# Handing sums of a two-level Strassen-Winograd matmul from PSUM bank to PSUM bank with ScalarE's copies, and two more products in quarters

## The chip, the cores and the metric

One core of one Trainium2 chip runs the whole kernel. The metric is the time of the device in microseconds; of the kernel before, three runs were timed, with a median of 1532.32 us (1531.6 to 1532.37). The core's engines are TensorE (PE, with its weight loads PEld), VectorE (DVE), ScalarE (ACT), GpSimd (POOL) and SyncE (SP). TensorE adds into PSUM, eight banks of 512 fp32 columns for each of 128 partitions.

## The reference

```python
m, k, n = 4096, 4096, 4096
a, b: float32, drawn from a normal distribution; alpha = 0.01
x = np.matmul(a, b)
return np.where(x > 0, x, alpha * x)
```

A product of two 4096 x 4096 matrices, and a leaky ReLU on the result, in fp32 in and out.

## The kernel before

The operands are rounded to fp16. The output is worked in sixteen regions of 1024 x 1024, named (g, j): g is the group of 1024 rows of A, j the group of 1024 columns of B. Region (0, 0) is an ordinary matmul, done while the inputs begin to arrive. The other fifteen follow one another in one loop, in the order (0,1), (0,2), (0,3), (1,2), (1,0), (1,3), (1,1), (2,2), (2,0), (2,3), (2,1), (3,2), (3,0), (3,1), (3,3). Each of them is a 2 x 2 block product over K = 2 x 2048, done in Winograd's form of Strassen's algorithm: seven products of [512 x 2048] by [2048 x 512] in place of eight. A row group's last region, where the next group's rows of A arrive, is called turning ((0,3), (1,1), (2,1)).

The seven products are in code `product(0)` to `product(6)`; here they are the first to the seventh. The list PRODUCTS names their operands: A11, A12, S2, S3, S1, A22, S4, where the S are sums of blocks of A, against blocks of B or sums T of them, which VectorE makes in place. A whole product is 64 matmuls of 128 x 512, over 16 chunks of K and 4 row tiles, each row tile adding in a PSUM bank. The first, third and fifth product add into the four banks y, which carry the running sum from one to the next. The second, fourth and sixth use the other four banks, z. The seventh adds onto y again. y and z change places from region to region.

What leaves a region:
- block C11 is the first product plus the second. ScalarE copies the first product out of y to SBUF (`keep`, giving u1), and VectorE adds the second product's banks to it. A leaky step follows and a store (`leave`).
- the third product's running sum is kept as u2, the fourth product as v. u2 + v and the fifth make the other blocks with the sixth and the seventh.

Many products are done once more by the same scheme, one level down, as seven "quarters": 7 x 16 matmuls of 128 x 256, 112 in all. These are the sixth and the seventh product of the ten regions that are neither of group 0 nor turning (`in_quarters`), the fourth of those among them that are not the first of their group (`in_fourth`) and of the turning ones of groups 1 and 2, and the fifth of the regions in the list FIFTH, which holds (2, 3) alone. The sums that the quarters need of a block of A are made once per row group, kept in DRAM (kept_q) and loaded again in each region; those of B are made by VectorE each time. The fourth, sixth and seventh quarters' results go from their bank to SBUF by ScalarE's copies and VectorE's adds (`more`, and the adds at line 1219).

The order of the work is written out by hand: within each engine and each queue instructions run in the order of the program text, and an engine that waits holds up all that is behind it. Semaphores between engines follow from the tiles: who writes or reads a bank waits for those before it that touch the same bank. These places matter below:
- Line 1101 and lines 1113 to 1116: regions in the list EARLY begin with one measurement of B (two in (2, 0) and (3, 1)). A measurement is four squares on ScalarE (line 231) and VectorE's additions of them (lines 240 to 243), with the fourth square and the next measurement waiting for VectorE to free a buffer. They stand in ScalarE's queue ahead of the first product's copies.
- `judge` (line 619) looks at what was measured. Its second half, some twelve small VectorE instructions, stands in the last region, (3, 3), ahead of the fifth product.
- `load_sums` (line 754) loads sums of A: on SP's queue for the sixth product, each into a buffer whose last reader must have ended; on ScalarE's queue, by `following`, for the seventh.
- `seventh_at_the_end` (line 992) is the last region's seventh product; its first quarter writes two banks at once, `one` and `one_more`, that is zbank + 3 and zbank + 1.
- `z6` at line 1271 gives the order in which the sixth product gets its banks; after a fifth in quarters it is (0, 2, 1, 3).

Of the kernel before, what the change touches and what calls it, by code (L numbers as in the profile page):

```python
# [31 lines left out]
MT = 4  # L32
# [16 lines left out]
def kernel(  # L49
# [17 lines left out]
    nc = tc.nc  # L67
# [274 lines left out]
    for what, i, *more in order:  # L342
        if what == "a":
            r, tiles = more
# [320 lines left out]
    FIFTH = {(2, 3)}  # L665
# [127 lines left out]
    for i, (g, j) in enumerate(regions):  # L793
# [14 lines left out]
        def product(n, banks, first):  # L808
# [26 lines left out]
        def fourth_in_quarters(banks, tq, sx):  # L835
# [11 lines left out]
            if not turning:  # L847
                quarter_product(sx[4], b[1, 1], into(other), True)
# [7 lines left out]
            if turning:  # L856
                quarter_product(sx[4], b[1, 1], into(other), True)
            return pairs, kept, [(block(r, n), pair(bank)) for r, n, bank in (
                (0, 0, fourth), (0, 1, other), (0, 1, third), (1, 0, one), (1, 1, one))]

# [43 lines left out]
        def sixth_in_quarters(pairs, banks, v_pairs, v, y, tq, sq, between=None):  # L904
# [4 lines left out]
            one, other, third, fourth = banks  # L909
# [13 lines left out]
            quarter_product(x[0, 0], b[0, 0], into(one), True)  # L923
            add(v[:2], y[:2])
            more(0, 0, one)
            add(v[2:], y[2:])
            quarter_product(sx(1), t(1), into(other), True)
            more(1, 1, other)
# [9 lines left out]
            more(0, 1, one)  # L938
            if between:

                leave(v_pairs, 1, 1, (0,))
                t3_of_b(y7)
            sums_of_b(y7, next_t, (2,))
            more(0, 0, fourth)
            quarter_product(sx(4), b[1, 1], into(other))
            following(1, sq.get("room"))
            next_t[4] = tq[2]
            more_t4 = lambda: sums_of_b(y7, next_t, (4,))
            if not between:
                more_t4()  # L950
            more(0, 1, other)
            quarter_product(sx(3), b[0, 1], into(one))
            following(3, sq.get("last"))
            more(1, 0, one)
            more(1, 1, one)
            quarter_product(x[1, 1], t(4), into(third), True)
            if between:
                more_t4()
            more(1, 0, third)
# [162 lines left out]
        u1_pairs, u1 = keep(y, side)  # L1122
# [23 lines left out]
        product(1, z, True)  # L1146
# [5 lines left out]
        add(u1, z)  # L1152
# [3 lines left out]
        if in_fourth:  # L1156
            tq = {n: new_a16() for n in (2, 4)}
# [7 lines left out]
            sums_of_b(quarters_of_b(i, 0, 1), tq, (4,))  # L1165
# [21 lines left out]
        if in_fourth:  # L1187
            tq[1] = t[:, 3]
            sums_of_b(quarters_of_b(i, 0, 1), tq, (1,))
# [21 lines left out]
        if in_fourth or turning and g:  # L1211
            v_pairs, v, parts = fourth_in_quarters(z, tq, {**s3_rooms(g), 4: a_quarter(sx4)})
            if turning:
                for n in range(3):
                    turn_a_in(0, 1, n)
            for n, (to, bank) in enumerate(parts):
                if in_fifth and n == 2:
                    sums_of_b(quarters_of_b(i, 0, 0), t5, (1,))
                nc.vector.tensor_add(to, bank, to)
                if in_fifth and n == 0:  # L1220

                    t3_of_b(quarters_of_b(i, 0, 0))
                    sums_of_b(quarters_of_b(i, 0, 0), t5, (2, 4))
            if turning or in_fifth:
                add_v()
        else:
# [84 lines left out]
        if not in_quarters:  # L1311
            product(5, z, g > 0)
            add(u2[::-1], z[::-1])
# [115 lines left out]
```

## Time and profile before

| | |
|---|---|
| median of three runs | 1532.32 us (1531.6 to 1532.37) |
| span of the profiled execution | 1531.4 us, 21934 instructions |
| TensorE: matmuls | 8715 |
| VectorE busy | 1171.2 us (76%) |
| ScalarE busy | 428.1 us (28%) |
| granted TensorE clock over the span | 1.000 |
| HBM read, written | 347.61 MB, 117.44 MB |

The profiled execution is read by its span, from the first to the last instruction; 0.9 us lie between that span and the median of the runs. PE is the matmul, L819 a whole product's and L762 a quarter's; L832 is ScalarE's copy out of a bank, L1041 VectorE's add of a bank to kept sums, L917 the sixth product's adds, L231 a square, L754 a load of sums of A. A row of the timeline has the start and the length in us, the engine, the line, the operation with its tiles and shapes and how many were merged; in brackets stands how long the engine had been idle before and what ended that. The chain of waits has start, length and what was on it. In the table of groups stand the busy time, the mean of one in ns, then the idle time before them and what ended it.

### The profile page before, as it was taken

What the parts mean: (1) busy time and instruction counts of PE and PEld (TensorE: products, weight loads), DVE (VectorE), ACT (ScalarE), POOL (GpSimd) and SP (SyncE); (2) the same over time, 40 slices, a digit from 0 to 9 for tenths busy, and PEclk for the clock granted to TensorE, in tenths of its full rate; (3) what the DMA queues carried; (4) which work ended last, traced back from release to release, by engine and by line L of the source; (5) the groups of instructions that cost most, each with busy time, mean ns of one, the idle gap of its engine ahead of it and who ended that gap; (6) DMA issues with size and microseconds to landing.
All of it is one profiled execution on the core that took longest, in us unless ns stands there. A gap on an engine that the chain in (4) does not pass through costs nothing. (4 is left out here: it accounts for less than half of the span.)

```text
span 1531.4 us, 21934 instructions
## 1 busy us (share of the span) xinstructions
PE 1521.0 (99%) x8715; PEld 851.5 (56%) x8715; DVE 1171.2 (76%) x1231; ACT 428.1 (28%) x734; POOL 258.2 (17%) x426
## 2 busy tenths in 40 slices
PE   9999999999999999999999999999999999999998
PEld 4444444444446567574544747577544475746656
DVE  4378867766897676768789599688978868687677
ACT  2201334646310213103651130313464103041210
POOL 5641110143202011022220001000331100101000
PEclk9999999999999999999999999999999999999999
DMA  9999995998979999899898939859999892948824
GB/s 248 188 216 200 239 281 168 180 193 176 251 312 257 277 237 276 243 290 246 184 310 279 302 149 231 294 154 343 217 241 297 229 347 70 295 161 189 302 97 140
DMA packets 194258, 356.50 MB, mean 233 GB/s; under 512 B 18913, under 2 KB 132833, under 8 KB 181090
## 3 DMA queue, kind: packets, MB, share of 16 engines
q0 software_dynamic: 119808, 112.22, 46.4%
q1 hardware_dynamic: 67714, 217.22, 38.0%
q10 hardware_dynamic: 6624, 25.56, 4.4%
q8 instruction: 70, 1.15, 0.3%
q14 instruction: 42, 0.34, 0.1%
HBM read 347.61 MB, written 117.44 MB: 304 GB/s over the span
## 5 line engine op out<-in xcount | busy, mean ns | idle before, releaser
L819 PE MATMUL ps<-b,a 128*128 128x512 f16 x2624 | 570.7, 379 | 1.4 <-DMA b<-in_b_dram 1.4
L819 PE MATMUL ps<-b,s 128*128 128x512 f16 x2176 | 475.2, 379 | 0.0
L819 PEld LDWEIGHTS <-a 128*128 128x128 f16 x2624 | 256.7, 98 | 309.3 <-issue 1.7
L819 PEld LDWEIGHTS <-s 128*128 128x128 f16 x2176 | 212.8, 98 | 255.2 <-issue 0.4
L592 DVE TENSOR_TENSOR b<-b 128x4096 f16<-128x4096 f16 x104 | 234.8, 2286 | 46.0 <-DMA b<-in_b_dram 34.1
L536 POOL DMA_DIRECT2D b<-in_b_dram x128 | 94.8, 745 | 879.8 <-PE ps L762 448.2
L832 ACT COPY c<-ps 128x512 f32<-128x512 f32 x164 | 85.0, 596 | 483.2 <-PE ps L819 439.2
L142 DVE STREAM_TRANSPOSE a<-a 128x512 uint32<-128x512 uint32 (+2 forms) x120 | 127.0, 1105 | 78.9 <-DMA a<-in_a_dram 78.9
L133 POOL DMA_DIRECT2D a<-in_a_dram x252 | 137.4, 553 | 245.5 <-ACT junk L611 73.6
L762 PEld LDWEIGHTS <-q 128*128 128x128 f16 x1488 | 145.6, 98 | 16.9
L313 DVE SCALAR_TENSOR_TENSOR c<-c 128x1024 f32<-128x1024 f32 (+2 forms) x123 | 141.8, 1194 | 4.1 <-ACT c L832 3.8
L611 ACT ACTIVATE junk<-a 128x512 bf16<-128x512 f16 x192 | 121.1, 631 | 83.4 <-DMA a<-in_a_dram 78.1
L1041 DVE TENSOR_TENSOR c<-ps,c 128x512 f32<-128x512 f32 x140 | 87.5, 683 | 62.8 <-PE ps L819 51.2
L231 ACT ACTIVATE sq<-b 128x2048 bf16<-128x2048 f16 x64 | 118.4, 1910 | 38.8 <-DVE sq L240 31.0
L762 PEld LDWEIGHTS <-a 128*128 128x128 f16 x1200 | 117.4, 98 | 17.4
L283 PE MATMUL ps<-b,a 128*128 128x512 f16 x512 | 112.2, 379 | 0.5 <-ACT a L380 0.2
L762 PE MATMUL ps<-b,q 128*128 128x256 f16 x816 | 95.6, 273 | 0.0
L762 PE MATMUL ps<-b,a 128*128 128x256 f16 x752 | 88.3, 273 | 0.0
L283 PEld LDWEIGHTS <-a 128*128 128x128 f16 x512 | 49.7, 98 | 60.8 <-issue 1.4
L977 ACT COPY c<-ps 128x512 f32<-128x512 f32 x9 | 5.3, 586 | 255.6 <-PE ps L762 145.8
L762 PEld LDWEIGHTS <-s 128*128 128x128 f16 x672 | 65.7, 98 | 7.6
L762 PE MATMUL ps<-q,q 128*128 128x256 f16 x544 | 64.6, 273 | 0.0
(108 smaller groups left out, 917.0 us busy)
## 6 DMA issues: line engine op xcount, KB each, us to landing
b<-in_b_dram POOLq DMA_DIRECT2D x136, 512.0 KB, 11.8
out_dram<-c SPq DMA_DIRECT2D x240, 256.0 KB, 7.0
a<-in_a_dram POOLq DMA_DIRECT2D x244, 128.0 KB, 5.7
b<-kept_half SPq DMA_DIRECT2D x28, 1024.0 KB, 11.8
b<-kept SPq DMA_DIRECT2D x20, 1024.0 KB, 8.8
q<-kept_qs ACTq DMA_DIRECT2D x40, 512.0 KB, 7.8
s<-kept_s SPq DMA_DIRECT2D x18, 1024.0 KB, 7.6
q<-kept_qa SPq DMA_DIRECT2D x28, 512.0 KB, 7.5
```

The source lines that it names most:

```text
L133: nc.gpsimd.dma_start(a16[32 * q:32 * q + 32], src.rearrange("(g i) w -> i g w", i=32))
L142: nc.vector.transpose(part.rearrange("p c m e -> p c (m e)").bitcast(U32) .rearrange("p c (g i) -> p g c i", i=32), src[:, :, i * n:(i + 1 ...
L231: nc.scalar.activation(to, self.parts[n], SQUARE)
L283: nc.tensor.matmul(ps, a_cols(at[0, h, u], c, mt, (h, u) == (0, 0)), bt[0, u, nt][:, c, :], start=first, stop=last,)
L313: nc.vector.scalar_tensor_tensor(t, t, alpha, t, op0=MULT, op1=MAX if alpha <= 1 else MIN)
L536: nc.gpsimd.dma_start(t[:, c:c + 4, :], b_rows(j, u, c, 4, nt, g > 0))
L592: nc.vector.tensor_tensor(f(to), f(x0), f(x1), op)
L611: nc.scalar.activation(junk, piece[:, q, :], SQUARE, accum_out=to[:, 4 * n + q:4 * n + q + 1])
L762: nc.tensor.matmul(to[m], xq[:, c // 2, rows, c % 2], yq[:, c, :], start=first and c == 0 and m < banks, stop=c == KC - 1, skip_group_chec ...
L819: nc.tensor.matmul(banks[mt], a_cols(t, c, mt, t is first_a), B(half, nt, k)[:, c, :], start=first and (k, c) == todo[0], stop=(k, c) == t ...
L832: nc.scalar.copy(kept[mt], banks[mt])
L1041: nc.vector.tensor_add(to, bank, to)
```

## The change

- `FIFTH` becomes (2, 3), (3, 1), (3, 3): the fifth product of two more regions is done in quarters. With it go, as in group 2, the sums of S1 in region (3, 0), their stores and loads, and in (3, 3) the second half of `judge` comes after the fifth product.
- C11: ScalarE copies the first product's banks y into the banks z, and the second product adds onto them; the whole block is then kept by ScalarE's copies. VectorE's four adds go. The last sixteen matmuls of the first product and the first sixteen of the second are ordered by bank.
- The fourth product in quarters of the regions `in_fourth` becomes `fourth_by_seeds`: sums that several blocks share are copied by ScalarE from bank to bank, and the quarters that follow add onto the copy. VectorE's adds at the end go from five to two, and T's sums 1 and 4 change places in time. The turning regions keep `fourth_in_quarters`.
- The sixth product in quarters is reordered and seeded in the same way: two copies into bank `one`, one into `other`; VectorE's `more` go from eight to six; the order of the quarters, of the loads for the seventh and of VectorE's sums changes.
- In the turning regions of groups 1 and 2 ScalarE copies u2 (with v in it) into z, the sixth product adds onto it, and ScalarE copies it back.

```diff
-    FIFTH = {(2, 3)}
+    FIFTH = {(2, 3), (3, 1), (3, 3)}
...
             order = [(mt, k, c) for k, c in todo for mt in range(MT)]
+            if n == 0:
+                order[-16:] = [(mt, k, c) for mt in range(MT) for k, c in todo[-4:]]
+            elif n == 1:
+                order[:16] = [(mt, k, c) for mt in range(MT) for k, c in todo[:4]]
             if n == 0 and late_s2:
...
+        def fourth_by_seeds(banks, tq, sx):
...
+            chain, shared, one, other = banks
...
+            quarter_product(x[0, 0], b[0, 0], into(chain), True)
+            nc.scalar.copy(one, chain)
+            quarter_product(sx[1], t(1), into(shared), True)
+            quarter_product(sx[2], t(2), into(chain))
+            nc.scalar.copy(other, chain)
+            quarter_product(x[0, 1], b[1, 0], into(one))
+            nc.scalar.copy(block(0, 0), pair(one))
+            quarter_product(sx[3], b[0, 1], into(chain))
+            nc.scalar.copy(one, chain)
+            nc.scalar.copy(block(1, 1), pair(chain))
+            quarter_product(sx[4], b[1, 1], into(other))
+            nc.scalar.copy(block(0, 1), pair(other))
+            quarter_product(x[1, 1], t(4), into(one))
+            nc.scalar.copy(block(1, 0), pair(one))
+            return pairs, kept, [(block(r, 1), pair(shared)) for r in (1, 0)]
...
         def sixth_in_quarters(...)
-            one, other, third, fourth = banks
+            chain, shared, one, other = banks
...
+            quarter_product(x[0, 0], b[0, 0], into(chain), True)
+            nc.scalar.copy(one, chain)
+            add(v, y)
+            quarter_product(sx(1), t(1), into(shared), True)
             following(4)
             next_t[2] = tq[1]
-            quarter_product(x[0, 1], b[1, 0], into(fourth), True)
             if between:
                 next(between)
+                leave(v_pairs, 1, 1, (0,))
+                t3_of_b(y7)
             else:
                 leave(v_pairs, 1, 1)
-            quarter_product(sx(2), t(2), into(one))
+            quarter_product(sx(2), t(2), into(chain))
+            nc.scalar.copy(other, chain)
             following(2)
+            sums_of_b(y7, next_t, (2,))
+            quarter_product(x[0, 1], b[1, 0], into(one))
+            more(0, 0, one)
+            next_t[4] = tq[2]
+            if not between:
+                sums_of_b(y7, next_t, (4,))
+            for r in (0, 1):
+                more(r, 1, shared)
+            quarter_product(sx(3), b[0, 1], into(chain))
+            nc.scalar.copy(one, chain)
+            more(1, 1, chain)
+            following(1, sq.get("last"))
+            quarter_product(sx(4), b[1, 1], into(other))
             if between:
+                sums_of_b(y7, next_t, (4,))
             more(0, 1, other)
+            following(3, sq.get("room"))
+            quarter_product(x[1, 1], t(4), into(one))
             more(1, 0, one)
...
-        u1_pairs, u1 = keep(y, side)
+        for mt in range(MT):
+            nc.scalar.copy(z[mt], y[mt])
...
-        product(1, z, True)
+        product(1, z, False)
...
-        add(u1, z)
+        u1_pairs, _ = keep(z, side)
...
+            if in_fifth:
+                t3_of_b(quarters_of_b(i, 0, 0))
+                sums_of_b(quarters_of_b(i, 0, 0), t5, (2, 4, 1))
...
             if turning or in_fifth:
                 add_v()
+            if turning:
+                z = [new_bank(zbank + mt) for mt in range(MT)]
+                for mt in range(MT):
+                    nc.scalar.copy(z[mt], u2[mt])
...
-            product(5, z, g > 0)
-            add(u2[::-1], z[::-1])
+            product(5, z, False)
+            if g:
+                for mt in range(MT):
+                    nc.scalar.copy(u2[mt], z[mt])
+            else:
+                add(u2[::-1], z[::-1])
```

More of the change, by code (lines that the diff above doesn't have):

```diff
@@ L943, in sixth_in_quarters @@
[L943 to L950, printed above, removed]
+            sums_of_b(y7, next_t, (2,))
[4 more added lines that the diff above has]
+                sums_of_b(y7, next_t, (4,))
@@ L954, in sixth_in_quarters @@
+            quarter_product(x[1, 1], t(4), into(one))
             more(1, 0, one)
[L955 to L959, printed above, removed]
             next_t[1] = tq[4]
@@ L1211 @@
         if in_fourth or turning and g:
-            v_pairs, v, parts = fourth_in_quarters(z, tq, {**s3_rooms(g), 4: a_quarter(sx4)})
+            fourth = fourth_by_seeds if in_fourth else fourth_in_quarters
+            v_pairs, v, parts = fourth(z, tq, {**s3_rooms(g), 4: a_quarter(sx4)})
             if turning:
```

34 lines of the change are left out of this document (10 added, 24 removed).

## The prediction

> **What bounds the kernel now.** I read the busy times first, then the chain that ended last.
>
> ```profile
> PE 1521.0 (99%) x8715; PEld 851.5 (56%) x8715; DVE 1171.2 (76%) x1231; ACT 428.1 (28%) x734; POOL 258.2 (17%) x426
> ```
>
> ```profile
> 945.38 33.41 DMA b<-in_b_dram
> 978.79 0.04 issue
> ...
> 1303.03 13.81 PE ps L819 x64
> 1316.85 24.45 PE ps L762 x224
> 1341.30 41.44 PE ps L819 x192
> ```
>
> TensorE is the bound, and a busy share that counts pipelined matmuls would prove little; the chain does. After one wait for a load of B, ended at 978.79, it is TensorE alone up to the last additions: a whole product takes 13.81 us for 64 matmuls (0.2158 each), two in quarters 24.45 us, so 12.23 us each and 1.747 us per quarter. The reader is to see that nothing else is on the path, so VectorE's 1171 us and ScalarE's 428 us cost nothing today. Work taken from VectorE therefore gives nothing by itself. What counts is how many matmuls go, and whether a new wait stops TensorE.
>
> **The change part by part.**
>
> *Two more fifth products in quarters.* In regions (3, 1) and (3, 3), 64 matmuls of 512 columns become 112 of 256: 2 × (13.81 − 12.23) = **−3.2 us**. This is the only work taken from TensorE. What it adds elsewhere (four sums of S1 on VectorE and their stores in region (3, 0), four sums of B and some ten small adds in each of the two regions, about 8 MB of copies) lies beside TensorE, whose cover is the whole products 3 and 5 around it; costed at nothing. Without that cover it would cost its VectorE time, about ten microseconds a region.
>
> *C11 handed on, the ordinary seam.* ScalarE now copies the first product's four banks into the second product's, and the second product adds onto them. Before, TensorE went from one to the other with no such wait. The new order ends bank m of the first product 4 matmuls (0.86 us) before bank m + 1 and begins the second product in the same way; where the fourth sum is loaded late the first two banks end 3.45 us early as they do now. Four copies fit:
>
> ```profile
> L832 ACT COPY c<-ps 128x512 f32<-128x512 f32 x164 | 85.0, 596 | 483.2 <-PE ps L819 439.2 <-DMA out_dram<-c 27.7 <-issue 16.3
> ```
>
> ```profile
> 917.70 2.05 ACT L832 COPY c<-ps 128x512 f32<-128x512 f32 x4 [20.18 <-PE ps L819]
> 512.58 1.91 ACT L231 ACTIVATE sq<-b 128x2048 bf16<-128x2048 f16 x1 [1.79 <-DVE sq L240]
> 514.45 1.07 ACT L832 COPY c<-ps 128x512 f32<-128x512 f32 x2
> ```
>
> At 0.51 us a copy against 0.86 us a bank nothing is lost as long as ScalarE is free some 0.7 us before the first product ends. The long idle time ahead of L832, most of it waiting for TensorE, says that it usually is. A region with one measurement queued ahead, (1, 0), is free at 514.5, 3.4 us before its seam at 517.9. Copies into a bank are not in the trace; nearest are these, into SBUF, of equal size. I take 0.60 us; half-width copies (about 0.37) and VectorE's adds of a bank (0.69) are the ends, so ±0.2 us per late seam. Cost at thirteen seams: nothing, and what hides it is an idle ScalarE. If that cover is gone, it costs the whole lateness:
>
> *C11 handed on, regions (2, 0) and (3, 1).* Two measurements of B stand in ScalarE's queue ahead of the copies: eight squares, broken by VectorE's additions.
>
> ```profile
> 876.60 21.75 PE L819 MATMUL ps<-b,a 128*128 128x512 f16 x100
> ```
>
> ```profile
> 877.76 5.52 ACT L231 ACTIVATE sq<-b 128x2048 bf16<-128x2048 f16 x3
> 885.07 1.91 ACT L231 ACTIVATE sq<-b 128x2048 bf16<-128x2048 f16 x1 [1.79 <-DVE sq L240]
> 888.27 7.31 ACT L231 ACTIVATE sq<-b 128x2048 bf16<-128x2048 f16 x4 [1.29 <-DVE sq L243]
> 895.49 1.05 ACT L832 COPY c<-ps 128x512 f32<-128x512 f32 x2
> ```
>
> In (2, 0) the first product starts at 876.60 and the second at 876.60 + 13.81 = 890.41. The first copy starts at 895.49. Today TensorE runs on, because the copy only evacuates; then it must wait for 895.49 + 0.60 = 896.1: **+5.7 us**. The later banks follow faster than they are needed. In (3, 1) the same:
>
> ```profile
> 1341.14 23.04 PE L819 MATMUL ps<-b,a 128*128 128x512 f16 x106
> ```
>
> ```profile
> 1342.30 5.52 ACT L231 ACTIVATE sq<-b 128x2048 bf16<-128x2048 f16 x3
> ...
> 1358.90 2.02 ACT L832 COPY c<-ps 128x512 f32<-128x512 f32 x4
> ```
>
> 1358.90 + 0.60 against 1341.14 + 13.81 = 1354.95: **+4.6 us**. Bound from below: the eight squares back to back (5.52 + 1.91 + 7.31 = 14.74 us after their start) would still be 2.7 us late in each region. Nothing excludes that VectorE comes sooner, nothing in the diff moves it: its adds of the seventh product and the first additions of the squares keep their places. I take the rows as they are.
>
> *The second product's evacuation* (keep of z after it) adds four copies on ScalarE and drops four adds on VectorE. The banks are used again one product later, so 13.81 us cover it. In turning regions squares of arriving rows of A stand ahead of it, and the seeds of the sixth product (u2 into z) and its copies back stand behind such squares too; cover is again a whole product, and I found no row that uses it up. Nothing.
>
> *The fourth product by seeds.* Copies sit one quarter (1.747 us) ahead of their use and take 0.6 us; five VectorE adds become two. ScalarE ends the four copies of the third product about 1.6 us into the fourth, before the first seed is due at 1.75. Nothing, with a slack of only about half a microsecond after the first seed.
>
> *The sixth product by seeds, after a fifth in quarters.* Two things move. The product of sx(3) goes from sixth to fifth place, so its operand is due 1.747 us sooner; its load cannot start before the fifth product has ended, since it takes the room of that product's last operand. And the second copy out of bank one must wait for VectorE's add of that bank (more(0, 0)), which now stands behind the adds to v, one sum, one leaky step, and two more sums.
>
> ```profile
> 1036.09 1.91 PE L762 MATMUL ps<-b,a 128*128 128x256 f16 x16
> ```
>
> ```profile
> L754 SPq DMA_DIRECT2D q<-kept_qa x1: 320/320/320, 1036.3 to 1036.3; - x1
> DMA to landing us min/median/max: 7.8/7.8/7.8
> ```
>
> ```profile
> 1037.15 1.29 DVE L902 TENSOR_TENSOR ps<-ps,a 128x512 f32<-128x512 f32 x2
> 1038.35 1.28 DVE L1041 TENSOR_TENSOR c<-ps,c 128x512 f32<-128x512 f32 x2
> 1039.54 0.68 DVE L917 TENSOR_TENSOR c<-ps,c 128x512 f32<-128x512 f32 x1
> ...
> 1041.93 1.22 DVE L694 TENSOR_TENSOR q<-b,q 128x2048 f16<-128x2048 f16 x1
> ...
> 1043.89 1.22 DVE L313 SCALAR_TENSOR_TENSOR c<-c 128x1024 f32<-128x1024 f32 x1
> 1045.02 1.22 DVE L686 TENSOR_TENSOR b<-b 128x2048 f16<-128x2048 f16 x1
> 1046.27 1.23 DVE L692 TENSOR_TENSOR q<-b 128x2048 f16<-128x2048 f16 x1
> 1047.42 1.88 DVE L917 TENSOR_TENSOR c<-ps,c 128x512 f32<-128x512 f32 x3
> ```
>
> In (2, 3) the sixth product starts at 1036.09, the load lands at 1036.3 + 7.8 = 1044.1, and the fifth quarter is due at 1036.09 + 4 × 1.747 = 1043.08: **+1.0 us**. The page's median for these loads,
>
> ```profile
> q<-kept_qa SPq DMA_DIRECT2D x28, 512.0 KB, 7.5
> ```
>
> gives 0.2 + 7.5 − 7.0 = **+0.7 us** in (3, 1); the ends are 0 and 1.5. VectorE, from the start of the sixth product: free at 2.26, four adds 2.4, then steps of 1.13, 1.13, 1.25, 1.15 and the add itself 0.69, done at 10.0; copy 10.6; due at 6 × 1.747 = 10.5. That 0.1 hides behind the late operand.
>
> *Region (3, 3), last.* Its fifth product is now in quarters, so the judging of the statistics moves on VectorE from ahead of a whole fifth product to between the fifth and the sixth:
>
> ```profile
> 1496.61 0.59 DVE L633 TENSOR_REDUCE most<-line 1x2 f32<-1x256 f32 x1
> ...
> 1499.65 0.15 DVE L640 TENSOR_TENSOR good<-ok 1x1 int32<-1x1 f32 x1
> ```
>
> That is 3.2 us more in the queue: more(0, 0) ends at 10.0 + 3.2 = 13.2, the copy at 13.8, and the last quarter, due at 10.5, ends at 13.8 + 1.75 = 15.5. Then the final product needs both its banks at once, zbank + 3 and zbank + 1, which in this bank order are the sixth's last two to be read. VectorE reaches the end of those reads after three adds (1.8), one sum (1.1) and two adds (1.2): 13.2 + 4.1 = 17.3, against 12.2 without waits: **+5.1 us**. The least is 0.9: the last bank can only be read after the last quarter has ended, and an add is 0.69 plus the 0.2 until it starts. The judging is all that fills the rest. In region (2, 3) the load of B that ended at 978.79 keeps its lead and its wait.
>
> Sum against the profiled span: 1531.4 − 3.2 + 5.7 + 4.6 + 1.0 + 0.7 + 5.1 = 1545.3. The median of the runs, 1532.32, stands 0.9 above that span, so **1546.2 us**, 0.9% slower. A difference under 0.2% (3.1 us) is about what cannot be told from no change.
>
> **The rivals.**
>
> *Faster: the squares no longer stand ahead of the copies in time.* If ScalarE reached the copies 0.7 us before the first product's end in (2, 0) and (3, 1), the path would be TensorE alone and only −3.2 (and the waits around a sixth product) would be left; with those hidden too, 1529.1. It decides at a chain of squares shorter by 5.7 and 4.6 us. Against it: even without any VectorE wait the squares are 2.7 us too long, and the diff moves no square. 4%, including no difference that can be measured.
>
> *The last region doesn't wait.* If the judging's 3.2 us and the bank order cost only their least, 0.9, the sum is 4.2 lower: 1542.0. For it: these waits are counted through ten queue steps, and today VectorE has room there. 15%.
>
> *The clock falls in the new gaps.*
>
> ```profile
> 1.19 4.11 PE L106 MATMUL wp<-w 128*128 128x512 f16 x11 [1.19 <-DVE x L92]
> 5.13 0.39 PE L373 MATMUL turned<-ident,a_rounded 128*128 128x128 f16 x4
> ```
>
> At the start eleven matmuls take 5.13 − 1.19 = 3.94 us instead of 11 × 0.2158 = 2.37, so a cold start costs 1.57 us. If each gap over three microseconds brings that back, one to three falls add 1.6 to 4.7: 1547.8 to 1550.9. The chain shows no gap that long before the end, so it speaks neither way. The Trainium skill, page TensorE: Matmul & The Clock Gate, section What's actually happening, says that the array goes back to half clock after at least one idle window of about 3.4 us; by that rule the wait in (2, 0) and perhaps that in (3, 1) would be paid twice over in part. No run here shows it yet. 25%.
>
> **How the numbers follow.** Forecast 50%, the clock 25%, the last region 15%, not slower 4%, and 6% for waits that I did not find, which lie above. The two early waits at their least (2.7 each) would give 1541.3, or 1537.1 with the last region at its least. The range 1539 to 1553 takes in these but for the last, the clock's three falls, and two microseconds beyond. Slower by over 0.2%: 0.95; within: 0.02; faster: 0.03.
>
> **What would show it.** Right: TensorE idle before the second product of (2, 0) and (3, 1), released by ScalarE's copy, with squares just ahead; before the fifth quarter of the sixth product in (2, 3) and (3, 1), released by a load; and in (3, 3) before the last quarter and the final product, released by ScalarE and VectorE. Fifth products of 12.23 us in (3, 1) and (3, 3). Matmuls of double spacing behind a gap would speak for the clock. Wrong: no gap at those seams, or gaps at ordinary ones, which would mean that the copies' 0.86 us per bank don't suffice.

## The result, and the profile after

The changed kernel takes 1575.01 us (median of 4 runs, 1574.05 to 1576.51); the kernel before, on the same chip, 1532.34 us. The ratio is 1.0277, with a 95% interval of 1.0263 to 1.0292: 2.8% slower, where 0.9% was forecast and the range ended at 1553. The profiled execution has a span of 1574.5 us and itself took 1576.51. Against the span before (1531.4) that is 43.1 us more.

Busy times on the page of the changed kernel, with the share of the span and the number of instructions:

```profile
PE 1531.3 (97%) x8811; PEld 863.8 (55%) x8811; DVE 1129.2 (72%) x1154; ACT 500.5 (32%) x869; POOL 258.1 (16%) x426
```

VectorE lost 42 us of work and ScalarE gained 72. TensorE got 96 more matmuls of half the width and 10.3 us more busy time, although two products became cheaper; its share fell from 99% to 97%. So it now waits, and some of its work got slower.

The waits of TensorE grouped by line and by what ended them; the numbers are the sum in us, how often, and the longest. In the changed kernel line 823 is the matmul of a whole product and 762 still that of a quarter; 1145 is C11's copies, 972 the sixth product's second copy into bank `one`, 942 its adds. First before, then after:

```profile
PE ps L819 <- DMA b<-in_b_dram: 1.4, 1, 1.4
```

```profile
PE ps L823 <- DMA b<-in_b_dram: 19.2, 6, 7.4
PE ps L823 <- ACT ps L1145: 11.8, 4, 5.5
PE ps L762 <- ACT ps L972: 3.2, 1, 3.2
...
PE ps L762 <- DVE c L942: 0.7, 1, 0.7
```

Two further gaps are short, in the fourth product of (2, 1) and in the sixth of (2, 3). These views give the idle time. What a wait costs is the distance from matmul to matmul less that of undisturbed ones, which is some 0.16 us more than the idle time (5.70 for 5.54); where the text says that a wait costs or loses something, it is this. So measured, the two short gaps are 0.69 and 0.29 us, and all fourteen sum to 37.9 us, against 1.6 before. The account of the 43.1 is then: waits +36.3, the two fifth products −3.2, matmuls that ran slowly behind the longer gaps +10.4, and −0.4 for the start, the end and rounding. The slow matmuls are the clock, below. Loads of B are the largest item, 20.2 us, and the forecast had nothing for them.

Two loads of B in the chain of waits after, start and length in us:

```profile
953.82 41.96 DMA b<-in_b_dram
...
1338.79 43.31 DMA b<-in_b_dram
```

The load that took 33.41 us of the chain before (2, 3) now takes 41.96, and one of 43.31 us, which was not on the chain at all, has appeared before (3, 1). The places of the waits in TensorE's timeline, in (2, 0), (2, 3), (3, 1) and (3, 3); in brackets is how long TensorE had been idle and what ended that:

```profile
897.51 5.72 PE L823 MATMUL ps<-b,a 128*128 128x512 f16 x19 [5.54 <-ACT ps L1145]
980.09 5.34 PE L823 MATMUL ps<-b,a 128*128 128x512 f16 x24 [1.11 <-DMA b<-in_b_dram]
986.50 1.89 PE L823 MATMUL ps<-b,a 128*128 128x512 f16 x8 [1.07 <-DMA b<-in_b_dram]
995.83 4.54 PE L823 MATMUL ps<-b,a 128*128 128x512 f16 x12 [7.44 <-DMA b<-in_b_dram]
1366.26 5.34 PE L823 MATMUL ps<-b,a 128*128 128x512 f16 x24 [2.33 <-DMA b<-in_b_dram]
1375.50 3.28 PE L823 MATMUL ps<-b,a 128*128 128x512 f16 x8 [3.90 <-DMA b<-in_b_dram]
1382.14 6.83 PE L823 MATMUL ps<-b,a 128*128 128x512 f16 x24 [3.36 <-DMA b<-in_b_dram]
1393.23 8.09 PE L823 MATMUL ps<-b,a 128*128 128x512 f16 x24 [4.26 <-ACT ps L1145]
1552.56 3.50 PE L762 MATMUL ps<-q,a 128*128 128x256 f16 x16 [3.23 <-ACT ps L972]
1556.84 3.54 PE L762 MATMUL ps<-b,s 128*128 128x256 f16 x31 [0.67 <-DVE c L942]
```

The waits for ScalarE's copies in (2, 0) and (3, 1) cost 5.70 and 4.42 us, against 5.7 and 4.6 forecast, and the squares stand ahead of the copies as the prediction had it. ScalarE's timeline, in (2, 0) and then in (3, 1):

```profile
889.67 7.31 ACT L231 ACTIVATE sq<-b 128x2048 bf16<-128x2048 f16 x4 [1.29 <-DVE sq L243]
896.88 2.03 ACT L1145 COPY ps<-ps 128x512 f32<-128x512 f32 x4
...
1382.18 1.91 ACT L231 ACTIVATE sq<-b 128x2048 bf16<-128x2048 f16 x1 [4.79 <-DMA b<-in_b_dram]
1385.38 7.31 ACT L231 ACTIVATE sq<-b 128x2048 bf16<-128x2048 f16 x4 [1.29 <-DVE sq L243]
1392.60 2.03 ACT L1145 COPY ps<-ps 128x512 f32<-128x512 f32 x4
```

In (3, 1), however, a square (1382.18) and the first product (1382.14) set off again together, both behind a late load of B. The rows that the prediction subtracted no longer set the length of this wait, so its nearness to 4.6 is chance; C11 alone, below, has the seam as forecast. New is that both first products, in (2, 3) and in (3, 1), stop three times each for loads of B: 9.6 us of idle time each.

Stretches of the changed kernel behind such gaps (the stretch, its length, busy time and instructions of PE, PEld, DVE, ACT and POOL, the granted TensorE clock, the DMA share, GB/s):

```profile
898.00:901.00 3.00, 3.00 (x10) 1.09 (x9) 2.83 (x9) 0.91 (x2) 0.00 (x0) 0.59 0.00 0
904.00:907.00 3.00, 3.00 (x16) 1.35 (x15) 3.00 (x2) 0.00 (x0) 0.00 (x0) 1.00 0.80 289
996.00:999.00 3.00, 3.00 (x8) 1.03 (x7) 1.20 (x1) 0.00 (x0) 0.00 (x0) 0.50 0.75 314
1394.00:1397.00 3.00, 3.00 (x8) 1.03 (x7) 2.86 (x8) 0.63 (x2) 0.00 (x0) 0.50 0.00 0
1553.00:1555.00 2.00, 2.00 (x11) 1.40 (x10) 1.90 (x4) 0.00 (x0) 0.00 (x0) 0.50 0.90 291
```

Behind the gaps of 5.54, 7.44, 4.26 and 3.23 us the clock is 0.50 to 0.59: eight matmuls of 512 columns in 3 us instead of fourteen. At 904, 6.5 us after the end of the first gap, it is back at 1.00. That is time which counts as busy and brings little progress. By the distance from matmul to matmul six such falls cost 10.4 us: 1.4 in (2, 0), 1.8 in (2, 3), 1.4, 1.5 and 2.8 in (3, 1) behind 3.90, 3.36 and 4.26 us, and 1.6 in (3, 3).

Why the loads of B are late shows in GpSimd's queue, which issues them as soon as the buffer's last reader is done. Region (2, 0), before and then after; the fourth product starts at 918.15 before and at 926.59 after:

```profile
918.15 2.02 PE L762 MATMUL ps<-b,a 128*128 128x256 f16 x17
```

```profile
924.09 1.48 POOL L536 DMA_DIRECT2D b<-in_b_dram  x2 [70.00 <-PE ps L762]
931.08 1.48 POOL L536 DMA_DIRECT2D b<-in_b_dram  x2 [5.52 <-PE ps L762]
```

```profile
926.59 1.58 PE L762 MATMUL ps<-b,a 128*128 128x256 f16 x13
```

```profile
936.02 2.99 POOL L536 DMA_DIRECT2D b<-in_b_dram  x4 [80.54 <-PE ps L762]
```

Two loads go out 5.9 us (924.09 − 918.15) into the fourth product before, and two more at 12.9. After, nothing goes out until 9.4 us, and then all four. In the old order the quarter with b11, `sx[4]`, comes third and frees one of the block's two buffers early. By seeds b11 is read sixth and b01 fifth, so both are held nearly to the end. (Lower-case b11 and b01 are `b[1, 1]` and `b[0, 1]`, quarters of the block at hand.)

These loads bring the next region's B12. What its first product waits for is B11, whose loads stand behind them in the same queue and go out no later than before, the last two 26.5 us into the fourth product both times:

```profile
944.65 1.48 POOL L536 DMA_DIRECT2D b<-in_b_dram  x2 [5.43 <-PE ps L819]
```

```profile
953.09 1.48 POOL L536 DMA_DIRECT2D b<-in_b_dram  x2 [5.43 <-PE ps L823]
```

So a late release of one block delays another. The last load of B12 lands 2.4 us later than before (34.7 us into the fourth product, not 32.3), the last of B11 8.5 us later. The other 6 us arise while B11 is loaded beside the transfers of other queues; which of these takes them was not tried by itself.

### The profile page after: what moved, and what is told of

The parts are those of the page before. It is cut to its first block, busy times and chain, and to the rows that moved or that the text cites. A ratio compares the mean times of both kernels' runs of the same rounds, so it can differ in the third digit from the quotient of the medians.

```text
span 1574.5 us, 22269 instructions
## 1 busy us (share of the span) xinstructions
PE 1531.3 (97%) x8811; PEld 863.8 (55%) x8811; DVE 1129.2 (72%) x1154; ACT 500.5 (32%) x869; POOL 258.1 (16%) x426
## 4 chain that ended last, share of the span: by engine, by line
PE 85%; DMA 8%; DVE 4%; ACT 2%; issue 1%; POOL 0%; SPq 0%; ACTq 0%; POOLq 0%; DVEq 0%
PE ps L823 60%; PE ps L762 19%; PE ps L283 7%; DMA b<-in_b_dram 5%; DMA a<-in_a_dram 1%; ACT sq L231 1%; DMA b<-kept_half 1%; DVE c L1063 0%; DVE c L313 0%; DVE ps L906 0%; DVE q L692 0%; DMA a_in<-in_a_dram 0%; DVE q L694 0%; DVE ps L927 0%; DVE q L696 0%
## 5 line engine op out<-in xcount | busy, mean ns | idle before, releaser
L823 PE MATMUL ps<-b,a 128*128 128x512 f16 x2624 | 581.1, 383 | 31.1 <-DMA b<-in_b_dram 19.2
L823 PE MATMUL ps<-b,s 128*128 128x512 f16 x2048 | 447.2, 379 | 0.0
L836 ACT COPY c<-ps 128x512 f32<-128x512 f32 x164 | 84.0, 599 | 310.9 <-PE ps L823 310.9
L762 PEld LDWEIGHTS <-q 128*128 128x128 f16 x1616 | 158.1, 98 | 18.4
L231 ACT ACTIVATE sq<-b 128x2048 bf16<-128x2048 f16 x64 | 118.8, 1911 | 54.4 <-DVE sq L240 34.7
L283 PE MATMUL ps<-b,a 128*128 128x512 f16 x512 | 112.2, 379 | 0.5 <-ACT a L380 0.2
L762 PE MATMUL ps<-b,q 128*128 128x256 f16 x880 | 103.3, 273 | 0.0
L1063 DVE TENSOR_TENSOR c<-ps,c 128x512 f32<-128x512 f32 x72 | 44.6, 681 | 58.8 <-PE ps L823 47.5
L1145 ACT COPY ps<-ps 128x512 f32<-128x512 f32 x60 | 32.1, 573 | 170.1 <-PE ps L823 170.1
L762 PE MATMUL ps<-q,q 128*128 128x256 f16 x656 | 75.9, 273 | 0.0
```

The lines of the kernel that those rows point to most:

```text
L231: nc.scalar.activation(to, self.parts[n], SQUARE)
L283: nc.tensor.matmul(ps, a_cols(at[0, h, u], c, mt, (h, u) == (0, 0)), bt[0, u, nt][:, c, :], start=first, stop=last,)
L762: nc.tensor.matmul(to[m], xq[:, c // 2, rows, c % 2], yq[:, c, :], start=first and c == 0 and m < banks, stop=c == KC - 1, skip_group_chec ...
L823: nc.tensor.matmul(banks[mt], a_cols(t, c, mt, t is first_a), B(half, nt, k)[:, c, :], start=first and (k, c) == todo[0], stop=(k, c) == t ...
L836: nc.scalar.copy(kept[mt], banks[mt])
```

## The experiments

**C11 alone.** The fifth, fourth and sixth product as before.

```diff
+            if n == 0:
+                order[-16:] = [(mt, k, c) for mt in range(MT) for k, c in todo[-4:]]
+            elif n == 1:
+                order[:16] = [(mt, k, c) for mt in range(MT) for k, c in todo[:4]]
...
-        u1_pairs, u1 = keep(y, side)
+        for mt in range(MT):
+            nc.scalar.copy(z[mt], y[mt])
...
-        product(1, z, True)
+        product(1, z, False)
...
-        add(u1, z)
+        u1_pairs, _ = keep(z, side)
```

> Of the change this kernel has only C11: the first product's banks copied by ScalarE into the second product's, and the ordered seams. Theory 1 (each term is its own): the gaps before the second product of (2, 0) and (3, 1), 5.7 and 4.4 us, of (2, 2) and (3, 2), 1.2 each, come from C11 alone, 12.5 us, and the fall of the clock behind the two long ones adds 1.5 to 4; the wait for B in (2, 3) stays near 1.6 and none arises in (3, 1): about 1532.3 + 15 = 1547. Theory 2 (the late loads of B follow from ScalarE's and VectorE's new timing): waits of some 10 us for B in (2, 3) here too: about 1557.

1548.6 us, ratio 1.0104 (1.0087 to 1.0121). Waits of TensorE:

```profile
PE ps L823 <- ACT ps L1127: 12.0, 4, 5.5
```

By the distance from matmul to matmul the four seams cost 5.70 us in (2, 0), 4.56 in (3, 1) and 1.19 each in (2, 2) and (3, 2). The slow clock behind the two long ones adds 2.74 and 1.69. No load of B is late. In (2, 1) the fourth product loses 1.79 us to one of VectorE's sums of B, which no forecast had. So this part alone costs what the forecast gave for the two long seams (10.3 us, here 10.26), and beside them 2.4 us at two seams that it had at nothing and 4.4 of clock that it had under a rival.

**The fifth products alone.**

```diff
-    FIFTH = {(2, 3)}
+    FIFTH = {(2, 3), (3, 1), (3, 3)}
```

> Of the change this kernel has only the two more fifth products in quarters, with the sums of S1 in (3, 0). Theory 1 (the late B comes from the order of the fourth product, which holds the next region's buffer longer): TensorE's wait for B in (3, 1) is at most 2 us, as in (2, 3) before, and the time is 1532.3 - 3.2 + 1.6 and some 2 us in (3, 3) for the judging, about 1532 to 1533. Theory 3 (the sums of S1 and their stores, 2 MB, fill the DMA queues in (3, 0)): the wait in (3, 1) is about 10 us with this part alone: about 1542.

1538.51 us, ratio 1.0036 (1.0024 to 1.0049): slower, although it takes 3.2 us from TensorE. Loads of B cost 2.14 us in (2, 3) and 1.31 in (3, 1), far from a large wait. The rest is lost in the last region. TensorE's timeline there:

```profile
1507.93 1.91 PE L762 MATMUL ps<-q,q 128*128 128x256 f16 x16 [1.88 <-DVE c L917]
...
1515.58 0.28 PE L762 MATMUL ps<-b,s 128*128 128x256 f16 x1 [0.46 <-DVE c L917]
1519.11 6.32 PE L762 MATMUL ps<-b,s 128*128 128x256 f16 x31 [3.24 <-DVE c L917]
```

The first wait is inside the sixth product, the others are at the start of the seventh; all three are for VectorE's adds of line 917, which stand behind the judging. The slow clock behind them costs some 2.8 us. What VectorE has to do there behind a fifth in quarters, the judging included, thus costs more than the quarters save, with the old sixth product too.

**The fourth product alone**, by seeds, in the regions `in_fourth` and with the sums of T that it needs.

```diff
-            v_pairs, v, parts = fourth_in_quarters(z, tq, {**s3_rooms(g), 4: a_quarter(sx4)})
+            fourth = fourth_by_seeds if in_fourth else fourth_in_quarters
+            v_pairs, v, parts = fourth(z, tq, {**s3_rooms(g), 4: a_quarter(sx4)})
```

> Of the change this kernel has only the fourth product by seeds. Theory 1 (the order holds the second half of B12 until the sixth quarter instead of the third, so the first loads of the next region's B start 3.4 us later): the wait for B in (2, 3) grows from 1.6 to about 10 us, and the clock falls behind it: about 1532.3 + 8.6 + 1.8 = 1542.7; no other region waits. Theory 2 or 3: (2, 3) keeps its 1.6 us, 1532.

1545.98 us, ratio 1.0089 (1.0072 to 1.0106). TensorE's timeline in (2, 3):

```profile
987.66 4.55 PE L819 MATMUL ps<-b,a 128*128 128x512 f16 x13 [8.65 <-DMA b<-in_b_dram]
```

The wait for B is there with nothing else of the change. In (2, 1) the fourth product loses 1.68 us, in (2, 0) the sixth 0.62. In (3, 1) there is no wait for B.

**The sixth product alone**, with the seeds in the turning regions.

```diff
-            product(5, z, g > 0)
-            add(u2[::-1], z[::-1])
+            product(5, z, False)
+            if g:
+                for mt in range(MT):
+                    nc.scalar.copy(u2[mt], z[mt])
+            else:
+                add(u2[::-1], z[::-1])
```

The new `sixth_in_quarters` goes with it as a whole.

> Of the change this kernel has only the sixth product by seeds and the seeds of the turning regions. All theories: only (2, 3) has a fifth in quarters, without the judging; a gap of 0.3 us before its fifth quarter, 1532.3 to 1533. If the seeds themselves held TensorE up, gaps would stand in all ten sixth products: 10 us or more.

1533.74 us over ten runs, ratio 1.0013 (1.0000 to 1.0025). One gap of 0.29 us, in (2, 3); no load of B is late. The six adds in place of eight give no time, and the order costs next to none.

**One release moved in the kernel before.** Is it the time at which b11 is let go, or is it ScalarE's copies and the new sums? The old fourth product, with its `sx[4]` quarter last:

```diff
             quarter_product(x[0, 0], b[0, 0], into(one), True)
             nc.scalar.copy(block(0, 0), pair(one))
-            if not turning:
-                quarter_product(sx[4], b[1, 1], into(other), True)
...
             quarter_product(sx[3], b[0, 1], into(one))
-            if turning:
-                quarter_product(sx[4], b[1, 1], into(other), True)
+            quarter_product(sx[4], b[1, 1], into(other), True)
```

> The kernel before with one quarter moved: in the fourth product of the regions that don't turn, sx[4] times B's (1, 1) quarter stands last, as in the turning ones, instead of third. No seeds, no other change. Theory 1 (what counts is when the fourth product lets go of B12's buffers, into which the next region's B is loaded): the first release moves from the third quarter to the sixth, 1.7 us later still than by seeds, and the wait for B in (2, 3) is 8.6 us or more: 1543 to 1548. Rival 1b (the seeds' other sides, earlier stores of S1 and loads of sums): the wait stays near 1.6 us, 1532 to 1533.

1549.8 us, ratio 1.0104 (1.0087 to 1.0121). TensorE's waits for B in (2, 3), and GpSimd's issue, both in the timeline:

```profile
973.42 5.34 PE L819 MATMUL ps<-b,a 128*128 128x512 f16 x24 [1.97 <-DMA b<-in_b_dram]
...
989.58 2.72 PE L819 MATMUL ps<-b,a 128*128 128x512 f16 x6 [8.07 <-DMA b<-in_b_dram]
```

```profile
929.92 2.99 POOL L536 DMA_DIRECT2D b<-in_b_dram  x4 [75.24 <-PE ps L762]
```

One quarter in another place, without a copy, a seed or an add changed, makes the same four late issues, the first 11.2 us into the fourth product (it starts at 918.75), and 10.9 us of waits. The release is the cause; the new copies and sums are not needed for it. (2, 1) loses another 3.3 us in its fourth product here.

**All but the fourth product.** The rest of the change with the old `fourth_in_quarters` and its sums of T.

```diff
...
-            fourth = fourth_by_seeds if in_fourth else fourth_in_quarters
-            v_pairs, v, parts = fourth(z, tq, {**s3_rooms(g), 4: a_quarter(sx4)})
+            v_pairs, v, parts = fourth_in_quarters(z, tq, {**s3_rooms(g), 4: a_quarter(sx4)})
...
```

> The whole change but the fourth product by seeds, which stays in its old order. Theory 1: the waits for B in (2, 3) and (3, 1), 10.1 us each with the whole change, fall to 2 us or less each, with the slow clock behind them: 1575.0 - 16 to 18 and about 4 of clock: 1553 to 1557. Theory 3 (stores of S1 make the wait in (3, 1)): (3, 1) keeps some 10 us, 1563 to 1566.

1559.03 us, ratio 1.0170 (1.0150 to 1.0190). The waits for B:

```profile
PE ps L823 <- DMA b<-in_b_dram: 5.6, 2, 3.7
```

One is in (2, 3) and one in (3, 1). The seams cost 5.71, 5.91 and twice 1.19 us, (3, 3) 3.39 and 0.84. So the old fourth gives back 16.0 us (1575.0 − 1559.0), 13.6 of them in waits for B (19.2 − 5.6); the 3.67 us left in (2, 3) are more than the 2 expected. The seam in (3, 1) costs 5.9 us here and 4.4 in the whole change. In both a square and TensorE start again together behind the last load of B11; in the whole change the 24 matmuls from there to the seam then take 6.83 us at the fallen clock, here 5.34 (at 1366.53), and what TensorE loses there it waits less at the seam.

**The fourth and the fifth together.** In (3, 1) neither part alone made a wait of size. This is the kernel with the fourth product alone, and

```diff
-    FIFTH = {(2, 3)}
+    FIFTH = {(2, 3), (3, 1), (3, 3)}
```

> The fourth by seeds and the two fifth products, without C11 and the sixth. If the parts add, 1532.7 + 13.2 + 5.8 = 1551.7 with a wait for B in (3, 1) under 2 us. If late release and S1's stores need each other in (3, 0), (3, 1) waits 8 to 11 us, as (2, 3) does, and the time is 1560 to 1563.

1564.08 us, ratio 1.0202 (1.0185 to 1.0219), where the sum of the two alone is 1532.7 + 13.2 + 5.8 = 1551.7. Waits:

```profile
PE ps L819 <- DMA b<-in_b_dram: 19.1, 4, 8.8
```

They cost 8.95 us in (2, 3), about as with the fourth alone (8.81), and 1.77, 2.49 and 6.55 in (3, 1), where the parts alone had none and 1.31. The two need each other there. From issue to landing the last load of B11 takes 12.3 us in the kernel before, 14.3 with the fourth alone, 33.2 with the fifths alone and 42.6 with both: with the fifths, whose sums of S1 are stored in that time, the lead that hid a late release is used up, and the late release then shows. It moves the issue of B's loads onto the time when the sums of S1 are stored and the parts of A loaded. The DMA issues from (3, 0) into (3, 1), with size and the median time in us from issue to landing, of the kernel before and then of the whole change:

```profile
b<-in_b_dram POOLq DMA_DIRECT2D x8, 512.0 KB, 9.2
```

```profile
b<-in_b_dram POOLq DMA_DIRECT2D x8, 512.0 KB, 26.9
...
kept_qs<-q SPq DMA_DIRECT2D x4, 512.0 KB, 8.6
```

The queues while B is loaded (packets, MB, and the time of their packets as a share of 16 engines' time), again before and after:

```profile
q0 software_dynamic: 2560, 2.54, 119.7%
```

```profile
q1 hardware_dynamic: 707, 2.58, 68.6%
q0 software_dynamic: 709, 0.71, 41.5%
```

Before, GpSimd's queue q0 has the engines to itself (1309 to 1322 us) and a 512 KB load of B lands in 9.2 us. After (1330 to 1340) it shares them with SP's and ScalarE's q1 and sends 709 packets in 10 us, where it sent 2560 in 13; the loads take 26.9 us, the time behind earlier loads of their own queue included. (The shares add to over 100% because the times of packets overlap.) The Trainium skill, page DMA: Bandwidth & Descriptors, section Queues, rings and completion order, says that each DMA engine serves its queues in turn, packet by packet; the packet counts, 707 and 709, agree with that.

**The seams mended.** The whole change, with the copies of C11 ahead of the second measurement and of T2's loads on ScalarE's queue:

```diff
-        for n, m in enumerate(early):
-            if n:
-                m.begin()
+        for m in early[:1]:
             m.end()
+        for mt in range(MT):
+            nc.scalar.copy(z[mt], y[mt])
+        for m in early[1:]:
+            m.begin()
...
-        for mt in range(MT):
-            nc.scalar.copy(z[mt], y[mt])
...
+        for m in early[1:]:
+            m.end()
```

> The whole change, with C11's copies put ahead of the second measurement and of T2's loads on ScalarE's queue, and that measurement's additions put behind the sums of B. By my step for C11 the four gaps ahead of second products (5.7, 4.4 and twice 1.2) go, and with them the slow clock behind the first and part of it behind the second: 1575.0 - 12.5 - 1.5 to 4.2, 1558 to 1561. If another wait stands right behind the squares, less than half of that goes: 1568 or more.

1562.29 us, ratio 1.0186 (1.0169 to 1.0203). All four gaps at seams are gone, (2, 2) and (3, 2) too, at 12.7 us less than the change. The waits for B stay and cost 10.4 us in (2, 3) and 11.1 in (3, 1), and a wait of 1.3 us for the operand of the sixth product's fifth quarter appears in (2, 3). In (2, 2) the cause of the gap can be read from ScalarE's queue in the changed kernel:

```profile
797.30 0.33 ACTq L518 DMA_DIRECT2D b<-kept_t  x1
797.67 2.04 ACT L1145 COPY ps<-ps 128x512 f32<-128x512 f32 x4 [3.18 <-PE ps L823]
```

The second load of T2, at line 518, waits for the first product to end, since that product reads the buffer it fills; the copies stand right behind it and begin with the last bank done instead of with the first. One of the waits for B in (3, 1) is worth a look, with the windows behind it:

```profile
1366.85 1.89 PE L823 MATMUL ps<-b,a 128*128 128x512 f16 x8 [3.51 <-DMA b<-in_b_dram]
```

```profile
1367.00:1369.00 2.00, 1.74 (x8) 0.68 (x7) 0.22 (x1) 1.74 (x1) 0.00 (x0) 1.00 1.05 370
```

Behind 3.51 us of idle time the clock did not fall.

**The judging later.** The whole change, with the judging behind the sixth product in (3, 3), its answer read at the end, the banks in plain order, and, in all sixth products behind a fifth in quarters, the read of bank `other` one step earlier (not shown):

```diff
-            even = nc.values_load(good[0:1, 0:1], min_val=0, max_val=1)
...
+            even = nc.values_load(good[0:1, 0:1], min_val=0, max_val=1)
...
-            z6 = (0, 2, 1, 3)
+            z6 = range(MT) if final else (0, 2, 1, 3)
...
-            if final:
-                good = next(judged)
...
             tq, sq = sixth_in_quarters(u2_pairs, banks, v_pairs, v, y, tq, sq, between)
+            if final:
+                good = next(judged)
```

> The whole change, with the judging's second half put behind the sixth product's work on VectorE, its answer read at the end of the seventh product, and the sixth product of (3, 3) on its banks in plain order, its read of bank other one step earlier. By my step for (3, 3) the gaps of 3.4 and 0.8 us there go, with the 1.6 us of slow clock behind the first: 1575.0 - 5 to 6, 1569 to 1570. If the queue of VectorE alone makes that wait, without the judging, 0.5 us or less goes: 1574 to 1575.

1578.36 us, ratio 1.0292 (1.0277 to 1.0308): no better than the change. The gap in the sixth product fell from 3.39 to 0.28 us, and a new one arose inside the seventh, in TensorE's timeline, with the slow clock behind it in the windows:

```profile
1564.70 5.54 PE L762 MATMUL ps<-b,q 128*128 128x256 f16 x32 [2.58 <-DVE c L1028]
```

```profile
1566.00:1568.00 2.00, 2.00 (x13) 1.44 (x12) 1.71 (x5) 0.00 (x0) 0.00 (x0) 0.55 0.53 187
```

In VectorE's queue the judging now stands just ahead of the adds that this gap waits for. At neither of the two places has VectorE 3 us to spare; moved work moves the gap.

**The fifth and sixth products, with the judging late.** The old C11 and the old fourth, with the edits of the judging above; some of the lines that differ from the kernel before:

```diff
-    FIFTH = {(2, 3)}
+    FIFTH = {(2, 3), (3, 1), (3, 3)}
...
-            z6 = (0, 2, 1, 3)
+            z6 = range(MT) if final else (0, 2, 1, 3)
...
-            product(5, z, g > 0)
-            add(u2[::-1], z[::-1])
+            product(5, z, False)
```

> Only the two fifth products and the sixth by seeds, with the judging late as above; C11 and the fourth as before the change. If the causes found are all, what is left are waits for B of 2 us or less in (2, 3) and (3, 1): 1532.7 - 3.2 - 1.8 + 1 to 3, 1529 to 1531.5, a little faster than before. If S1's stores cost (3, 1) or (2, 3) more than 3 us, 1533 or more.

1539.7 us, ratio 1.0056 (1.0038 to 1.0074), slower than the kernel before where a gain was expected. A load of B costs 2.11 us in (3, 1), and the gap in the seventh product of (3, 3), where the judging stands ahead again, costs 2.75 us and the slow clock behind it.

**All but the fourth, seams mended and judging late.** The change with the old fourth and the two mendings above:

```diff
+            v_pairs, v, parts = fourth_in_quarters(z, tq, {**s3_rooms(g), 4: a_quarter(sx4)})
...
+        for m in early[:1]:
             m.end()
+        for mt in range(MT):
+            nc.scalar.copy(z[mt], y[mt])
...
+            z6 = range(MT) if final else (0, 2, 1, 3)
```

> The whole change without the fourth by seeds, with C11's copies ahead of the second measurement and of T2's loads, and with the judging late: C11 kept, its lateness removed. If C11 is free at seams where ScalarE is free, this is as fast as the kernel with the fifth and sixth alone, 1529 to 1533; the sums of S1 and earlier VectorE work leave waits for B of 2 to 6 us in (2, 3) and (3, 1), as in the kernel without the fourth, and then it is 1533 to 1537.

1541.74 us, ratio 1.0059 (1.0047 to 1.0071), above both times expected. No gap stands at any seam, but 2.58 us of idle time in (3, 3) and, in (3, 1), this wait in the timeline, behind which the clock is 0.50:

```profile
1353.46 4.87 PE L823 MATMUL ps<-b,a 128*128 128x512 f16 x14 [3.00 <-DMA b<-in_b_dram]
```

**C11 mended, and the sixth product.** The same without the two new fifths and with the judging where it was:

```diff
-    FIFTH = {(2, 3), (3, 1), (3, 3)}
+    FIFTH = {(2, 3)}
```

> What of the change showed no cost by itself or could be mended: C11 with its copies ahead of the second measurement and of T2's loads, and the sixth product by seeds. No more fifth products, the fourth as before. TensorE has the matmuls of the kernel before; if the causes found are all, no gap over 0.3 us is left at any seam, 1531 to 1534, not to be told from before. If C11's copies cost TensorE something at ordinary seams, 0.3 us at each of fifteen would make 1537.

1534.09 us, ratio 1.0014 (1.0004 to 1.0024). A wait of 1.7 us for B in (2, 3), where it was 1.4 before, and 0.29 in its sixth product are all that is left of TensorE's waits in these regions. No seam costs TensorE anything where ScalarE is free, and nothing is gained: the time is 1.5 us above the kernel before, with an interval that just leaves out no change. None of these kernels beats the kernel before. All twelve runs came out above the time that their expectation gave for what was then found, by 0.1 to 8.4 us, the most in two of those with the judging moved; so the prices above are not the whole cost.

## Why the prediction was wrong

The direction was right and the size was not: 1575.0 against 1546.2, outside the range. Some of its steps held and three did not, and a rival that it left out of its sum came on top.

- "In region (2, 3) the load of B that ended at 978.79 keeps its lead and its wait": this step failed, and with it "The fourth product by seeds … Nothing". The prediction weighed the reordered fourth product by what its quarters wait for, not by what they let go. The cover that it named was right (no seed of the fourth product shows as a wait of TensorE in the whole change), but the order of last use of b11 and b01 decides when GpSimd can issue the loads of B12, and those of B11 are behind them. In the whole change that load landed 8.5 us later against the fourth product, and TensorE idled 9.6 us in place of 1.4. The profile before had that wait of 1.4 us, the sign that this load has no slack. One quarter moved in the old kernel costs 16.3 us (release_late, 1549.8 against 1533.5), the fourth by seeds alone 13.2.
- Extra sums of S1 and their copies "costed at nothing": this failed in (3, 1). Alone they cost 1.3 us there; with the late release 10.8 in that region. The cover named, whole products beside them, is a cover for VectorE. It is none for the DMA queues: the last load of B11 took 33.2 us there with the fifths alone, 12.3 before.
- "Cost at thirteen seams: nothing": right at eleven. (2, 2) and (3, 2) cost 1.2 us each, because the prediction read ScalarE's queue for squares only and not for T2's DMA issues, which are also instructions of that queue.
- Seams of (2, 0) and (3, 1), +5.7 and +4.6: held, at 5.70 and 4.56 with C11 alone. In the whole change (3, 1) costs 4.42 by another way, behind the late load, so that agreement is luck. The copies from bank to bank, taken at 0.60 us, take 0.573, by the groups of the changed kernel:

```profile
L1145 ACT COPY ps<-ps 128x512 f32<-128x512 f32 x60 | 32.1, 573 | 170.1 <-PE ps L823 170.1
```

- The fifths, −3.2 us: held for TensorE's work. It gains nothing as long as the last region gives back more; the net of that part is +5.8.
- The sixth, +1.0 and +0.7: 0.29 and about 0. The loads of line 754 in that stretch land in a median of 6.6 us, where 7.8 and 7.5 had been taken, so TensorE did not wait for the operand. The 0.29 is the wait for the second copy into bank `one`, ahead of the last quarter, which the prediction had at 0.1 and hidden.
- Region (3, 3), +5.1: the gaps cost 3.39 + 0.84 = 4.2 us. The mechanism, judging ahead of the adds, held, and the slow clock behind the first gap came on top.
- The rival "The clock falls in the new gaps", one to three falls at 1.57 us each, happened, and more often, since the waits for B brought gaps that it didn't count. The falls cost 10.4 us, against its 4.7. The Trainium skill, page TensorE: Matmul & The Clock Gate, section What's actually happening, was weighed there by its figure of 3.4 us; the clock fell behind 5.54 and 7.44 us, but also behind 3.23 here and 2.58 and 3.00 in the experiments, and it did not fall behind 3.51 in seams_mended. So 2.58 us can be enough and 3.51 too little, and the measurement decides.

Term by term, forecast +13.9 against the span and measured +43.1: loads of B +18.6 more (20.2 − 1.6), the clock +10.4, the two other seams +2.4, the sixth, the fourth and (3, 3) together −1.6 (5.2 against 6.8), the two long seams −0.2, and −0.4 at the start, the end and in rounding.

## What to carry to other kernels

When the order of operations changes, list for each buffer when its last reader ends, and which prefetch waits for that; here a release 3.5 us later turned a wait of 1.4 us, for another block in the same queue, into one of 8.7 (the fourth alone). Read every queue that an engine issues, its DMAs included, ahead of a copy that moves onto the critical path. An engine that is idle for most of the span, like ScalarE here, is still late at the few places where its queue is full, and most gaps on TensorE of 2.6 us or more are paid a second time in clock.

## What the runs showed of the hardware

- The clock of TensorE fell to between 0.50 and 0.59 behind idle times of 2.58 us (0.55 in judged_late, 0.50 in no_fourth_mended) and more, and not behind 2.33 us in the changed kernel (1366.26) or 1.88 in fifth_alone. The length of the gap alone does not decide it: behind 3.51 us in seams_mended the clock stayed at 1.00. By the distance from matmul to matmul a fall cost 1.4 to 2.8 us in the changed kernel, on top of the gap.
- A software queue alone took 119.7% of sixteen engines' time in packets; beside a hardware queue at 68.6% it had 41.5%, with as many packets as the other (709 and 707), and its 512 KB loads took 26.9 us to landing instead of 9.2.
- ScalarE copies a bank to another bank (128 x 512, fp32) in 573 ns, no dearer than into SBUF (596 in the kernel before), and matmuls add onto the copy.
